# Both heads of a pair at once on TensorE: attention's value products and retention of a two-layer hybrid mixer

## Chip, cores and metric

The kernel runs on one core of one Trainium2 chip. The metric is the device time of one execution in microseconds (us).

## What is computed

A two-layer encoder over 512 tokens of width 1024, in fp32. Each layer is half a SwiGLU feed-forward network (FFN), then a mixer of four parallel groups of 256 channels (short convolution, an RWKV-7 recurrence in both directions, retention, latent attention) whose outputs w_out joins, then half of another FFN. The change touches retention and attention; both have 4 heads of 64 channels:

```python
# retention, per head: chunks qc, kc, vc of q, k (roped) and v
scores = jnp.einsum('bhnid,bhnjd->bhnij', qc, kc) * intra_decay[None, :, None]
o = jnp.einsum('bhnij,bhnjd->bhnid', scores, vc)
...
o = (o + dec_start * jnp.einsum('bhnid,nbhde->bhnie', qc, R_f)
     + dec_end * jnp.einsum('bhnid,nbhde->bhnie', qc, R_b))
...
# attention, per block of queries
sc = jnp.einsum('bqhd,bkhd->bhqk', qn, k_nope) + jnp.einsum('bqhr,bkr->bhqk', qr, k_rope)
p = jax.nn.softmax(sc.astype(jnp.float32) * scale, axis=-1)
return jnp.einsum('bhqk,bkhd->bqhd', p.astype(v.dtype), v)
```

## The kernel before

Activations lie with channels on the 128 partitions and the 512 tokens along the free axis. FFN and projections split each fp32 operand into two parts of a faster type and make three products (lines 338 to 340); the products inside the mixers are plain fp32 and go over the array twice.

`Mixers.run` writes a layer's mixer down as: RWKV's projections, its inverse, its recurrence (`rwkv_chain`, 8 steps of two chunks), attention's latents, the convolution, retention's projections, attention of heads 0 and 1 (`mla(0)`), retention, RWKV's norm, attention of heads 2 and 3 (`mla(1)`), w_out. A scheduler then orders each engine's instructions by priorities and by its own model of time; so the recurrence's short products (lines 1043 to 1107) are spread over the stretch, and PE does the other mixers' products between them. PE and the other engines take their instructions strictly in the order that results. `in_turn` ties a list of calls together so that they are issued in that order; the recurrence uses it to alternate between heads or directions that lie on different halves of the array.

A product of heads in retention or attention fills only a part of the 128x128 array. Retention works on heads 2j and 2j+1 (the pair j) in partitions 0 to 63 and 64 to 127. Its 512 tokens are two halves (c) of 256, each of two tiles (s) of 128. Per pair:

- keys are transposed (line 609) and scaled by decay on DVE (611); `ret_sp`, the states of both halves, is 8 products of 128 rows by 64 columns (619), copied to `st` (623);
- head by head, half by half: scores `ret_ps` (634), 2 products of 64 rows by 128 columns and 256 tokens; DVE multiplies by the decay (636) into `ret_ms`; into `ret_po` go the product of queries with the state (639, 64 rows by 64 columns) and two products of values with `ret_ms` (642, 128 rows by 64 columns, head e on column half e).

`mla` goes head by head too: scores `m_sc` (775), softmax on DVE and ACT (777 to 782), transposes `m_ptp` (787) to four tiles `m_pT` (788), then four products with values (792, 128 rows by 64 columns, 512 tokens) into `m_po`, copied to its half of `y` (793). The accumulators of a head's products (PSUM tiles) come from three tags: "mm" has 3 banks, "a" 2, "b" 3; retention uses "mm" alone, heads 2 and 3 of attention use all three. The tiles `m_pT` and `ret_ms` come from the pool "f" of 23.

Of the kernel before, what the change touches and what calls it, by code (L numbers as in the profile page):

```python
# [9 lines left out]
F32R = mybir.dt.float32r  # L10
# [5 lines left out]
P = 128  # L16
# [3 lines left out]
NT = T // P  # L20
# [7 lines left out]
MLA_TAGS = (("mm", "mm", "mm"), ("mm", "mm", "mm"), ("b", "a", "mm"), ("b", "a", "mm"))  # L28
H = 4
N = 64  # L30
# [382 lines left out]
class Mixers:  # L413
# [179 lines left out]
    def retention(self):  # L593
        k, l, nc, V, A, G = self.k, self.l, self.nc, self.nc.vector, self.nc.scalar, self.nc.gpsimd
        mm = nc.tensor.matmul
        q, kk, vv = self.rq, self.rk, self.rv
        kdt, _ = CON["kd"]
        outs = []
        for j in range(2):
# [8 lines left out]
            for tt in range(NT):  # L608
# [2 lines left out]
            V.tensor_tensor(kn.rearrange("p (t h d) -> p t h d", t=NT, h=2), pt.rearrange("p (t h d) -> p t h d", t=NT, h=2),  # L611
                            tab.unsqueeze(3).to_broadcast([P, NT, 2, N]), ALU.mult)
            sps = k.ps("ret_sp", "mm")
            for e in range(2):
                h = 2 * j + e
                for d in range(2):
                    for s in range(2):
                        tt = 2 * d + s
                        mm(sps[64 * e:64 * e + 64, N * d:N * d + N],
                           kn[:, P * tt + 64 * e:P * tt + 64 * e + 64], vv(tt)[:, N * h:N * h + N],  # L620
                           start=s == 0, stop=s == 1)
            st = big[:, 768:896]
            V.tensor_copy(st, sps[:, 0:2 * N])
            po = k.ps("ret_po", "mm")
            for e in range(2):
                h = 2 * j + e
                r = slice(64 * e, 64 * e + 64)
                for c in range(2):
                    i = slice(256 * c, 256 * c + 256)
                    ms = k.ft("ret_ms")  # L630
                    ps = k.ps("ret_ps", "mm")
                    for s in range(2):
                        jt = 2 * c + s
                        mm(ps[:, 256 * s:256 * s + 256], kk[j][r, P * jt:P * jt + P], q[j][r, i], start=True, stop=True)
                    for s in range(2):
                        V.tensor_tensor(ms[:, 256 * s:256 * s + 256], ps[:, 256 * s:256 * s + 256],
                                        toe[e][:, 128 - 128 * s:384 - 128 * s], ALU.mult)

                    mm(po[r, i], st[r, N * (1 - c):N * (1 - c) + N], qd[r, i], start=True, stop=False)
                    for s in range(2):  # L640
                        jt = 2 * c + s
                        mm(po[r, i], vv(jt)[:, N * h:N * h + N], ms[:, 256 * s:256 * s + 256],
                           start=False, stop=s == 1)
            o, sq = k.ft("ret_o"), k.ft("ret_sq")
            V.tensor_tensor(o, po, self.rg[j], ALU.mult)
            A.activation(sq, po, AF.Square)
# [113 lines left out]
    def mla(self, j):  # L760
        k, l, nc, V, A = self.k, self.l, self.nc, self.nc.vector, self.nc.scalar
        mm = nc.tensor.matmul
        ident = k.con("ident")
        fq, v = self.fq, self.mv
        for h in (2 * j, 2 * j + 1):
            e = h % 2
            if e == 0:
                y = k.ft("m_y")
            qT, kT = self.qT[h], self.kT[j][:, e]
            tag = MLA_TAGS[h]  # L770
            pp = [k.ht("m_p") for _ in range(2)]
# [12 lines left out]
            for kt in range(NT):  # L784
# [1 line left out]
                for qt in range(NT):  # L786
                    nc.tensor.transpose(pt[:, P * qt:P * qt + P], pp[qt // 2][:, qt % 2, P * kt:P * kt + P], ident)
                (A.copy if kt % 2 else V.tensor_copy)(pT[kt], pt)
            po = k.ps("m_po", tag[2])
            r = slice(64 * e, 64 * e + 64)  # L790
            for kt in range(NT):
                mm(po[r], v[:, kt, N * h:N * h + N], pT[kt], start=kt == 0, stop=kt == NT - 1)  # L792
            (A.copy if e else V.tensor_copy)(y[r], po[r])
            if e:
                k.dump(f"ymla{j}_{l}", y)
                self.y_split(6 + j, y, k.vt(f"ys{6 + j}", dt=F32R))


    def rwkv_in(self):
# [460 lines left out]
```

## Time and profile before

| | us |
|---|---|
| median of 3 runs | 2233.18 (2233.13 to 2240.66) |
| the profiled execution | 2230.46 |
| its span, first to last instruction | 2227.9 |
| PE busy | 2171.2 |
| DVE busy | 1142.5 |
| ACT busy | 696.0 |
| POOL busy | 193.5 |
| mean granted clock of TensorE | 0.987 |

PE does the matrix products and transposes, DVE and ACT work through tiles element by element, POOL is a third such engine and SP issues the DMAs. Busy times overlap; the span is the time from the first to the last instruction. The mixer's stretch of the first layer lies at some 370 to 760 us of the span, that of the second at some 1470 to 1860. An fp32 product stands as two rows (passes) in the trace, each with a weight load of its own.

### The profile page before, as it was taken

What the parts mean: (1) busy time and instruction counts of PE and PEld (TensorE: products, weight loads), DVE (VectorE), ACT (ScalarE), POOL (GpSimd) and SP (SyncE); (2) the same over time, 40 slices, a digit from 0 to 9 for tenths busy, and PEclk for the clock granted to TensorE, in tenths of its full rate; (3) what the DMA queues carried; (4) which work ended last, traced back from release to release, by engine and by line L of the source; (5) the groups of instructions that cost most, each with busy time, mean ns of one, the idle gap of its engine ahead of it and who ended that gap; (6) DMA issues with size and microseconds to landing.
All of it is one profiled execution on the core that took longest, in us unless ns stands there. A gap on an engine that the chain in (4) does not pass through costs nothing.

```text
span 2227.9 us, 27585 instructions
## 1 busy us (share of the span) xinstructions
PE 2171.2 (97%) x11332; PEld 1732.9 (78%) x11332; DVE 1142.5 (51%) x1905; ACT 696.0 (31%) x1035; POOL 193.5 (9%) x176
## 2 busy tenths in 40 slices
PE   8999999999999999999999999999999999999997
PEld 7888888777765888888888888887776568888886
DVE  4454345587467643443543344447856765344333
ACT  4322233432233422232322222334223243222232
POOL 1000001132110100000100000003121101000001
PEclk9999999989999999999999999999999999999998
DMA  4223224134002322332322232341340113223222
GB/s 166 95 96 108 95 94 148 59 95 131 15 16 71 128 95 84 105 104 77 103 95 95 94 105 95 110 131 60 95 113 15 63 49 122 94 86 113 95 84 77
DMA packets 65294, 204.68 MB, mean 92 GB/s; under 512 B 26512, under 2 KB 26768, under 8 KB 50960
## 3 DMA queue, kind: packets, MB, share of 16 engines
q1 hardware_dynamic: 65168, 202.93, 27.7%
q8 instruction: 88, 1.44, 0.3%
q14 instruction: 38, 0.31, 0.0%
HBM read 191.37 MB, written 9.44 MB: 90 GB/s over the span
## 4 chain that ended last, share of the span: by engine, by line
PE 84%; DVE 9%; DMA 2%; ACT 2%; SPq 1%; issue 1%; POOL 0%; DVEq 0%; ACTq 0%; POOLq 0%
PE pg L340 7%; PE pg L338 7%; PE pg L339 7%; PE pu L338 7%; PE pu L339 7%; PE pd L339 7%; PE pd L340 7%; PE pu L340 7%; PE pd L338 7%; DVE w_lo L328 2%; PE m_po L792 1%; DVE Rb L958 1%; PE po L338 1%; PE po L340 1%; PE pj L338 1%
## 5 line engine op out<-in xcount | busy, mean ns | idle before, releaser
L327 ACT CAST w_hi<-w_raw 128x1024 fp32r<-128x1024 f32 (+4 forms) x446 | 367.4, 836 | 1133.6 <-PE pg L339 309.2
L328 DVE TENSOR_TENSOR w_lo<-w_raw,w_hi 128x1024 fp32r<-128x1024 f32 (+4 forms) x446 | 434.1, 981 | 215.5 <-ACT w_hi L327 206.9
L338 PE MATMUL pg<-xg,w_hi 128*128 128x512 f32 x704 | 275.4, 391 | 6.0 <-ACT w_hi L327 6.0
L340 PE MATMUL pg<-xg,w_lo 128*128 128x512 f32 x704 | 274.9, 390 | 0.6 <-DVE w_lo L328 0.5
L339 PE MATMUL pg<-xg,w_hi 128*128 128x512 f32 x704 | 275.0, 391 | 0.0
L338 PE MATMUL pu<-xg,w_hi 128*128 128x512 f32 x704 | 274.1, 389 | 0.5 <-ACT w_hi L327 0.5
L339 PE MATMUL pu<-xg,w_hi 128*128 128x512 f32 x704 | 274.2, 389 | 0.0
L340 PE MATMUL pu<-xg,w_lo 128*128 128x512 f32 x704 | 274.1, 389 | 0.0
L340 PE MATMUL pd<-g,w_lo 128*128 128x512 f32 x704 | 273.9, 389 | 0.0
L338 PE MATMUL pd<-g,w_hi 128*128 128x512 f32 x704 | 273.9, 389 | 0.0
L339 PE MATMUL pd<-g,w_hi 128*128 128x512 f32 x704 | 273.9, 389 | 0.0
L372 DVE TENSOR_TENSOR g<-pu,s 128x512 f32<-128x512 f32 x88 | 60.8, 691 | 274.2 <-PE pu L340 271.4
L288 POOL TENSOR_TENSOR acc<-acc,sq 128x512 f32<-128x512 f32 x48 | 65.5, 1364 | 1521.7 <-ACT sq L286 1521.3
L369 DVE TENSOR_TENSOR s<-pg,rb 128x512 f32<-128x512 f32 x88 | 60.8, 691 | 206.4 <-PE pg L340 206.3
L340 PE MATMUL pj<-xg,w_lo 128*128 128x512 f32 x368 | 149.5, 408 | 13.4 <-DVE w_lo L328 13.3
L338 PEld LDWEIGHTS pg<-xg,w_hi 128*128 128x128 f32 x704 | 132.6, 188 | 33.9 <-ACT w_hi L327 6.2
L340 PEld LDWEIGHTS pg<-xg,w_lo 128*128 128x128 f32 x704 | 132.5, 188 | 29.0 <-DVE w_lo L328 1.8
L339 PEld LDWEIGHTS pg<-xg,w_hi 128*128 128x128 f32 x704 | 132.5, 188 | 28.5 <-DVE xg L274 1.0
L338 PEld LDWEIGHTS pu<-xg,w_hi 128*128 128x128 f32 x704 | 132.2, 188 | 28.2 <-ACT w_hi L327 0.9
L340 PEld LDWEIGHTS pu<-xg,w_lo 128*128 128x128 f32 x704 | 132.2, 188 | 27.6 <-DVE w_lo L328 0.3
L338 PEld LDWEIGHTS pd<-g,w_hi 128*128 128x128 f32 x704 | 132.2, 188 | 27.5
L339 PEld LDWEIGHTS pd<-g,w_hi 128*128 128x128 f32 x704 | 132.2, 188 | 27.5
(293 smaller groups left out, 2893.6 us busy)
## 6 DMA issues: line engine op xcount, KB each, us to landing
w_raw<-gu SPq DMA_DIRECT2D x87, 1024.0 KB, 4.9
w_raw<-dn SPq DMA_DIRECT2D x64, 704.0 KB, 4.1
w_raw<-win SPq DMA_DIRECT2D x22, 1024.0 KB, 5.0
w_raw<-wo SPq DMA_DIRECT2D x32, 256.0 KB, 2.8
xs<-x SPq DMA_DIRECT2D x16, 256.0 KB, 4.7
x<-xs SPq DMA_DIRECT2D x16, 256.0 KB, 5.4
w_raw<-wtv SPq DMA_DIRECT2D x4, 576.0 KB, 4.6
x<-xT SPq DMA_DIRECT2D x8, 256.0 KB, 5.7
```

The costliest lines, as they stand in the source:

```text
L288: nc.gpsimd.tensor_tensor(self.acc, self.acc, self.sq, ALU.add)
L327: self.split_hi = self.nc.scalar.copy(hi[:, s], raw[:, s])
L328: self.nc.vector.tensor_tensor(lo[:, s], raw[:, s], hi[:, s].bitcast(F32), ALU.subtract)
L338: T_.matmul(ps, hi, xh, start=start, stop=False)
L339: T_.matmul(ps, hi, xl, start=False, stop=False)
L340: T_.matmul(ps, lo, xh, start=False, stop=stop)
L369: V.tensor_tensor(s, pg, rb, ALU.mult)
L372: V.tensor_tensor(g, pu, s, ALU.mult)
L792: mm(po[r], v[:, kt, N * h:N * h + N], pT[kt], start=kt == 0, stop=kt == NT - 1)
L958: V.tensor_tensor(Rb[:, 0:t, t:], Rb[:, 0:t, t:], tm, ALU.subtract)
```

## The change

In retention the loops over the pair's heads go inside: the states (line 617 of the changed program), the scores (634) and the values (646) of both heads are issued alternately by `in_turn`, head 0 on one half of the array, head 1 on the other. Each head of the pair has its own bank of scores. The product of queries with the state is made for both heads at once (642), with the two states as diagonal blocks of a 128x128 matrix; POOL sets the other two blocks to zero (625), and DVE copies each head's state in an instruction of its own (626). In attention the value products of a pair (801) come after both heads' transposes and alternate between the heads; one copy of 128 partitions takes the place of two of 64.

```diff
-            for e in range(2):
-                h = 2 * j + e
-                for d in range(2):
-                    for s in range(2):
-                        tt = 2 * d + s
-                        mm(sps[64 * e:64 * e + 64, N * d:N * d + N],
-                           kn[:, P * tt + 64 * e:P * tt + 64 * e + 64], vv(tt)[:, N * h:N * h + N],
-                           start=s == 0, stop=s == 1)
-            st = big[:, 768:896]
-            V.tensor_copy(st, sps[:, 0:2 * N])
+            def state(d, s, e):
+                h, tt = 2 * j + e, 2 * d + s
+                return mm(sps[64 * e:64 * e + 64, N * d:N * d + N], kn[:, P * tt + 64 * e:P * tt + 64 * e + 64],
+                          vv(tt)[:, N * h:N * h + N], start=s == 0, stop=s == 1)
+
+            self.in_turn([(state, d, s, e) for d in range(2) for s in range(2) for e in range(2)])
+
+            st = big[:, 768:1024].rearrange("p (d e n) -> p d e n", d=2, e=2)
+            for e in range(2):
+                r = slice(64 * e, 64 * e + 64)
+                G.memset(st[r, :, 1 - e], 0.0)
+                V.tensor_copy(st[r, :, e], sps[r, 0:2 * N].rearrange("p (d n) -> p d n", d=2))
             po = k.ps("ret_po", "mm")
-            for e in range(2):
-                h = 2 * j + e
-                r = slice(64 * e, 64 * e + 64)
-                for c in range(2):
-                    i = slice(256 * c, 256 * c + 256)
-                    ms = k.ft("ret_ms")
-                    ps = k.ps("ret_ps", "mm")
-                    for s in range(2):
-                        jt = 2 * c + s
-                        mm(ps[:, 256 * s:256 * s + 256], kk[j][r, P * jt:P * jt + P], q[j][r, i], start=True, stop=True)
...
-                    mm(po[r, i], st[r, N * (1 - c):N * (1 - c) + N], qd[r, i], start=True, stop=False)
-                    for s in range(2):
-                        jt = 2 * c + s
-                        mm(po[r, i], vv(jt)[:, N * h:N * h + N], ms[:, 256 * s:256 * s + 256],
-                           start=False, stop=s == 1)
+            for c in range(2):
+                i = slice(256 * c, 256 * c + 256)
+                ps, ms = [k.ps("ret_ps", "mm") for _ in range(2)], [k.ft("ret_ms") for _ in range(2)]
+
+                def scores(s, e):
+                    r, jt = slice(64 * e, 64 * e + 64), 2 * c + s
+                    return mm(ps[e][:, 256 * s:256 * s + 256], kk[j][r, P * jt:P * jt + P], q[j][r, i], start=True, stop=True)
+
+                self.in_turn([(scores, s, e) for s in range(2) for e in range(2)])
+                for e in range(2):
...
+                mm(po[:, i], st[:, 1 - c].rearrange("p e n -> p (e n)"), qd[:, i], start=True, stop=False)
+
+                def values(s, e):
+                    h, jt = 2 * j + e, 2 * c + s
+                    return mm(po[64 * e:64 * e + 64, i], vv(jt)[:, N * h:N * h + N], ms[e][:, 256 * s:256 * s + 256],
+                              start=False, stop=s == 1)
+
+                self.in_turn([(values, s, e) for s in range(2) for e in range(2)])
...
-            po = k.ps("m_po", tag[2])
-            r = slice(64 * e, 64 * e + 64)
-            for kt in range(NT):
-                mm(po[r], v[:, kt, N * h:N * h + N], pT[kt], start=kt == 0, stop=kt == NT - 1)
-            (A.copy if e else V.tensor_copy)(y[r], po[r])
-            if e:
-                k.dump(f"ymla{j}_{l}", y)
-                self.y_split(6 + j, y, k.vt(f"ys{6 + j}", dt=F32R))
+            pTs.append(pT)
+
+        po = k.ps("m_po", MLA_TAGS[2 * j + 1][2])
+
+        def values(kt, e):
+            o = N * (2 * j + e)
+            return mm(po[64 * e:64 * e + 64], v[:, kt, o:o + N], pTs[e][kt], start=kt == 0, stop=kt == NT - 1)
+
+        self.in_turn([(values, kt, e) for kt in range(NT) for e in range(2)])
+        (A.copy if j else V.tensor_copy)(y, po)
+        k.dump(f"ymla{j}_{l}", y)
+        self.y_split(6 + j, y, k.vt(f"ys{6 + j}", dt=F32R))
```

The scheduler makes a new order of the whole stretch. Three places on PE's queue, in the first layer (a product is one row here, x3 is three equal ones in a row; lines behind the change are moved by up to ten).

From heads 0 and 1's last transposes to the first pair's first scores, before:

```order
L787 MATMUL m_ptp<-con_t,m_p 128x128 x4
L792 MATMUL m_po<-m_pT,m_v 64x512 x3
L609 MATMUL ret_pt<-con_t,ro_t 128x128 x4
L1089 MATMUL zy_3764<-ch_3762 64x64 x2
L1089 MATMUL zy_3765<-ch_3763 64x64 x2
L1089 MATMUL zy_3764<-ch_3762 64x64 x2
L1089 MATMUL zy_3765<-ch_3763 64x64 x2
L792 MATMUL m_po<-m_pT,m_v 64x512
L619 MATMUL ret_sp<-ret_v,ret_big 64x64 x8
L634 MATMUL ret_ps<-ro_t 128x256 x2
```

and now:

```order
L793 MATMUL m_ptp<-con_t,m_p 128x128 x4
L801 MATMUL m_po<-m_pT,m_v 64x512 x5
L609 MATMUL ret_pt<-con_t,ro_t 128x128 x4
L801 MATMUL m_po<-m_pT,m_v 64x512 x3
L1099 MATMUL zy_3764<-ch_3762 64x64 x2
L1099 MATMUL zy_3765<-ch_3763 64x64 x2
L1099 MATMUL zy_3764<-ch_3762 64x64 x2
L1099 MATMUL zy_3765<-ch_3763 64x64 x2
L617 MATMUL ret_sp<-ret_v,ret_big 64x64 x8
L634 MATMUL ret_ps<-ro_t 128x256 x4
```

Head 1's four value products were the rows of 3 and 1 (head 0's stood some 55 rows earlier); the eight of both heads are the rows of 5 and 3, and the scores are four, of both heads.

The first pair's two halves, from the product with the state to the next piece of the recurrence, before:

```order
L639 MATMUL ret_po<-ret_big 64x256
L634 MATMUL ret_ps<-ro_t 128x256 x2
L642 MATMUL ret_po<-ret_ms,ret_v 64x256 x2
L639 MATMUL ret_po<-ret_big 64x256
L634 MATMUL ret_ps<-ro_t 128x256 x2
L1062 MATMUL zy_3840<-Sd,KQ_2516 128x128
```

and now:

```order
L642 MATMUL ret_po<-ret_big 128x256
L646 MATMUL ret_po<-ret_ms,ret_v 64x256
L634 MATMUL ret_ps<-ro_t 128x256
L646 MATMUL ret_po<-ret_ms,ret_v 64x256 x3
L634 MATMUL ret_ps<-ro_t 128x256 x3
L642 MATMUL ret_po<-ret_big 128x256
L1072 MATMUL zy_3840<-Sd,KQ_2516 128x128
```

Four value products of a half stand as one and three, and so do the next half's scores.

Heads 2 and 3 at the start of w_out (`po`), from transposes of head 2 to the last value products, now:

```order
L793 MATMUL m_ptp<-con_t,m_p 128x128 x6
L256 MATMUL ret_pb<-con_t,ret_sq 128x128 x8
L801 MATMUL m_po<-m_pT,m_v 64x512
L793 MATMUL m_ptp<-con_t,m_p 128x128 x2
L1170 MATMUL py_5329<-con_t,gn_wk 128x128 x2
L338 MATMUL po<-ys_5178,w_hi 128x512 x2
L1170 MATMUL py_5330<-con_t,gn_wk 128x128 x2
L793 MATMUL m_ptp<-con_t,m_p 128x128 x8
L801 MATMUL m_po<-m_pT,m_v 64x512 x4
L339 MATMUL po<-ys_5178,w_hi 128x512
```

Before, their value products stood as four groups of 2, each behind its own transposes; now they are groups of 1, 4 and, ten products of w_out later, 3.

## Rows read from the trace of the kernel before

**Rows 1.** The page: the chain that ended last, by engine.

```profile
PE 84%; DVE 9%; DMA 2%; ACT 2%; SPq 1%; issue 1%; POOL 0%; DVEq 0%; ACTq 0%; POOLq 0%
```

**Rows 2.** Table by stage, first layer: start:end us, length, then as its heading says.

```profile
core 0: us, PE busy (x) PEld busy (x) DVE busy (x) ACT busy (x) POOL busy (x), PEclk, DMA share, GB/s
605.00:645.00 40.00, 39.93 (x345) 23.90 (x340) 26.24 (x65) 16.43 (x37) 5.63 (x12) 1.00 0.00 1
645.00:679.00 34.00, 33.36 (x275) 20.89 (x273) 23.01 (x61) 7.21 (x14) 7.12 (x7) 1.00 0.23 75
679.00:693.00 14.00, 10.38 (x32) 4.48 (x32) 13.62 (x51) 5.79 (x14) 1.32 (x1) 0.88 0.18 66
693.00:760.00 67.00, 66.92 (x296) 50.40 (x295) 42.40 (x72) 28.38 (x47) 9.66 (x7) 1.00 0.28 95
```

**Rows 3.** Waits of PE, 605 to 693 us: total us, times, longest us.

```profile
PE m_sc L775 <- ACT m_p L780: 3.5, 2, 3.2
PE zy L1107 <- DVE ch L1077: 0.6, 1, 0.6
```

**Rows 4.** By tile, both layers: ns of one (min/median/max), first and last start.

```profile
L792 PE MATMUL m_po<-m_pT,m_v x64: 592/592/643, 624.7 to 1813.1; 128*64 128x512 f32 x64
...
L634 PE MATMUL ret_ps<-ro_t x64: 376/376/480, 646.2 to 1770.3; 64*128 64x256 f32 x64
```

**Rows 5.** Timeline of PE: start us, us until its last end, line, shape, count.

```profile
644.80 0.59 PE L792 MATMUL m_po<-m_pT,m_v 128*64 128x512 f32 x1
...
645.23 0.59 PE L792 MATMUL m_po<-m_pT,m_v 128*64 128x512 f32 x1
645.24 1.05 PE L619 MATMUL ret_sp<-ret_v,ret_big 128*64 128x64 f32 x15
646.22 1.13 PE L634 MATMUL ret_ps<-ro_t 64*128 64x256 f32 x4
```

**Rows 6.** Timeline of PE, first pair of heads: one head's groups one after another.

```profile
649.11 1.13 PE L634 MATMUL ret_ps<-ro_t 64*128 64x256 f32 x4
650.17 1.08 PE L642 MATMUL ret_po<-ret_ms,ret_v 128*64 128x256 f32 x4
651.17 0.64 PE L639 MATMUL ret_po<-ret_big 64*64 64x256 f32 x2
651.75 1.13 PE L634 MATMUL ret_ps<-ro_t 64*128 64x256 f32 x4
```

**Rows 7.** Timeline of PE: groups that already alternate between two halves of the array.

```profile
631.55 0.69 PE L1089 MATMUL zy<-ch 128*64 128x64 f32 x16
632.16 1.99 PE L775 MATMUL m_sc<-m_kT,m_qT 128*128 128x512 f32 x4
...
635.85 1.16 PE L1043 MATMUL psG<-KQ,KB 64*128 64x128 f32 x16
636.94 0.71 PE L1062 MATMUL zy<-Sd,KQ 128*128 128x128 f32 x4
```

**Rows 8.** Timeline of PE: line 642 on one half of columns, line 619 on the other.

```profile
659.71 0.27 PE L619 MATMUL ret_sp<-ret_v,ret_big 128*64 128x64 f32 x1
659.74 0.38 PE L642 MATMUL ret_po<-ret_ms,ret_v 128*64 128x256 f32 x1
...
659.95 0.38 PE L642 MATMUL ret_po<-ret_ms,ret_v 128*64 128x256 f32 x1
...
660.17 0.38 PE L642 MATMUL ret_po<-ret_ms,ret_v 128*64 128x256 f32 x1
```

**Rows 9.** DVE and POOL in the first layer, by line and by tile.

```profile
L636 DVE TENSOR_TENSOR ret_ms<-ret_ps,ret_big 128x256 f32<-128x256 f32 x16 | 6.0, 416 | 3.7 <-PE ret_ps L634 3.7
...
L1099 DVE TENSOR_TENSOR Sd<-ch,Pm 128x256 f32<-128x256 f32 x4 | 1.7, 467 | 0.0
...
L623 DVE COPY ret_big<-ret_sp x2: 279/286/292, 646.3 to 661.2; 128x128 f32<-128x128 f32 x2
...
L1102 POOL TENSOR_TENSOR Sc<-ch,Pd 128x128 f32<-128x128 f32 x2 | 1.2, 612 | 7.7 <-DVE ch L1098 7.7
```

More of the change, by code (lines that the diff above doesn't have):

```diff
@@ L624, in retention @@
-            po = k.ps("ret_po", "mm")
-            for e in range(2):
-                h = 2 * j + e
-                r = slice(64 * e, 64 * e + 64)
-                for c in range(2):
-                    i = slice(256 * c, 256 * c + 256)
-                    ms = k.ft("ret_ms")
-                    ps = k.ps("ret_ps", "mm")
-                    for s in range(2):
-                        jt = 2 * c + s
-                        mm(ps[:, 256 * s:256 * s + 256], kk[j][r, P * jt:P * jt + P], q[j][r, i], start=True, stop=True)
-                    for s in range(2):
-                        V.tensor_tensor(ms[:, 256 * s:256 * s + 256], ps[:, 256 * s:256 * s + 256],
-                                        toe[e][:, 128 - 128 * s:384 - 128 * s], ALU.mult)
-                    mm(po[r, i], st[r, N * (1 - c):N * (1 - c) + N], qd[r, i], start=True, stop=False)
-                    for s in range(2):
-                        jt = 2 * c + s
-                        mm(po[r, i], vv(jt)[:, N * h:N * h + N], ms[:, 256 * s:256 * s + 256],
-                           start=False, stop=s == 1)
+            def state(d, s, e):
+                h, tt = 2 * j + e, 2 * d + s
+                return mm(sps[64 * e:64 * e + 64, N * d:N * d + N], kn[:, P * tt + 64 * e:P * tt + 64 * e + 64],
+                          vv(tt)[:, N * h:N * h + N], start=s == 0, stop=s == 1)
@@ new lines, in retention @@
+            self.in_turn([(state, d, s, e) for d in range(2) for s in range(2) for e in range(2)])
+            st = big[:, 768:1024].rearrange("p (d e n) -> p d e n", d=2, e=2)
+            for e in range(2):
+                r = slice(64 * e, 64 * e + 64)
+                G.memset(st[r, :, 1 - e], 0.0)
+                V.tensor_copy(st[r, :, e], sps[r, 0:2 * N].rearrange("p (d n) -> p d n", d=2))
+            po = k.ps("ret_po", "mm")
+            for c in range(2):
[6 more added lines that the diff above has]
+                for e in range(2):
+                    for s in range(2):
+                        V.tensor_tensor(ms[e][:, 256 * s:256 * s + 256], ps[e][:, 256 * s:256 * s + 256],
+                                        toe[e][:, 128 - 128 * s:384 - 128 * s], ALU.mult)
+                mm(po[:, i], st[:, 1 - c].rearrange("p e n -> p (e n)"), qd[:, i], start=True, stop=False)
[4 more added lines that the diff above has]
+                self.in_turn([(values, s, e) for s in range(2) for e in range(2)])
@@ L764, in mla @@
         fq, v = self.fq, self.mv
+        y = k.ft("m_y")
+        pTs = []
         for h in (2 * j, 2 * j + 1):
             e = h % 2
-            if e == 0:
-                y = k.ft("m_y")
             qT, kT = self.qT[h], self.kT[j][:, e]
```

## Prediction

> **What bounds the kernel now.** I read the chain of waits first: TensorE (PE) carries 84% of the chain that ended last [rows 1], so a microsecond of PE work is worth a microsecond wherever PE doesn't wait. Then the table by stage, for the stretch in which the changed products run. From 605 to 679 us PE is busy for 73.3 of 74 us, from 693 to 760 for 66.9 of 67, at a granted clock of 1.00 (2.4 GHz); only from 679 to 693 does it stand still, for 3.6 us, while DVE is busy for 13.6 of 14 us and the granted clock is 0.88 in the mean, so part of it 1.2 GHz after the standstill [rows 2]. PE's waits say the same: 0.6 us on DVE and 3.5 us on ACT's softmax between 605 and 693 us [rows 3]. So the recurrence's steps never wait for their own latency: other PE work, ours among it, fills every gap. The second layer repeats this some 1,100 us later. The reader is to see that this stretch is bound by the PE queue, with a softmax stall at its end that belongs to DVE and ACT.
>
> Next, what a product costs. An fp32 product makes two passes over the array: 16 value products a layer, in two layers, are 64 rows [rows 4]. A pass of 512 columns starts 0.43 us after the one before (644.80, 645.23) [rows 5]; one of 256 columns 0.215 us after (659.74, 659.95, 660.17) [rows 8]. A group of passes of another shape also pays for opening: four passes of line 634 hold PE for 1.06 us, four of 642 for 1.00, two of 639 for 0.58, against 0.86, 0.86 and 0.43 of passes, so 0.20, 0.14 and 0.15 us a group [rows 6].
>
> Last, whether two halves of the array do work at the same time here. Line 1089 alternates column halves: 16 passes of 64 columns take 0.61 us, 0.038 each, where line 619's 15 that don't alternate take 0.98, 0.065 each [rows 7, 5]. Line 1043 alternates row halves: 16 passes of 128 columns in 1.09 us, 0.068 each, where half of a 256-column pass would be 0.107 [rows 7, 8]. And line 642 on one column half keeps its 0.215 us while line 619 runs on the other [rows 8]. So a pair costs one pass. I call that a slot.
>
> **The change, part by part, for one layer.** The order of the changed program decides how many pairs are formed: the scheduler cuts groups of four into one and three. A lone product takes 2 slots, three alternating ones 4 (the half that has two of them decides), four take 4, five take 6.
> - Attention's values: 32 passes become groups of 5 and 3 (first pair of heads), and of 1, 4 and 3 (second), so 6+4+2+4+4 = 20 slots. 12 passes of 0.43 us go: 5.2 us, half of it after 693 us, where PE is just as full [rows 2].
> - Retention's scores: 32 passes become groups of 4, 1, 3, then 1, 3, 1, 3: 22 slots. Ten of 0.215 us: 2.2 us.
> - The product with the state (line 639): 8 products over a quarter of the array become 4 over all of it, 16 passes become 8: 1.7 us.
> - Retention's values: 32 passes become four times 1 and 3: 24 slots: 1.7 us.
> - The state (line 619): 1.0 us becomes line 1089's 0.6 for the first pair [rows 5, 7]; for the second it already ran half beside line 642 [rows 8], so nothing. 0.4 us.
> - Openings: 32 groups of these products become 24. Other groups (transposes, scores of the recurrence) are split in the new order; I count half of the eight, at 0.15 us: 0.6 us.
>
> Sum 11.8 us a layer, **23.6 us** in both.
>
> What it adds: one more DVE copy of 0.29 us for each pair of heads (two of 64 partitions for one of 128) and two memsets of zero blocks on POOL, bounded by nothing and by the nearest POOL row, 0.6 us each [rows 9]. The order puts at least the group of scores and a piece of the recurrence between them and the product that reads them, over 1.5 us of PE work, so I cost both at nothing; without that cover it would be 1.5 us a pair of heads, 6 us in all. Fewer evacuations of attention's output (two of 128 partitions a layer, not four of 64) save DVE and ACT some 0.6 us each, beside the PE work.
>
> What can be late next: the values wait for DVE's multiplies by the decay, 0.416 us each [rows 9], now four for both heads, 1.7 us, and behind them on PE's queue stands the recurrence. The scores of the second half also need the banks that the first two of these free. Before, one head's group ran while DVE worked on the other's. Between scores and values there now stand the product with the state, 0.6 us, and mostly a piece of the recurrence, 0.6 to 1.2 us. Uncovered rest: between nothing and 0.8 us in each of the 8 groups of both layers (two pairs, two halves). I take 0.15 us, nearer to nothing because PE never waited for such a multiply before: 1.2 us in all. Holding the first head's four transposed tiles until the second's are ready costs only space; its products move back behind the second head's transposes.
>
> Net: 22.4 us. The profiled execution took 2230.46 us, 2227.9 of them the span and 2.6 around it, so it would take 2208.1. It stands 2.7 us below the median of the runs shown, 2233.18; from that the forecast is **2211 us**. About 0.5%, 11 us, is what a measurement of this kernel can tell from no change.
>
> **One rule against the trace.** In the rows the weight loads of one column half don't hold up the other: line 642's passes keep their 0.215 us while line 619 starts a pass every 0.06 us beside them, each with a load of its own [rows 8]. The Trainium skill ("TensorE: Matmul & The Clock Gate", Part 3, packing small matmuls) states that a weight load overlaps matmuls in flight only where its row group differs. Both column halves use all rows, so by that rule the value products would gain nothing, and the time would be the second rival's. The trace does not agree with it, at least for short passes beside long ones; two long passes on two column halves stand in no row.
>
> **The rivals.**
> (1) DVE takes over. From 645 to 693 us it is busy for 36.6 of 48 us [rows 2]. If what PE gains there only lengthens the stall for the softmax and the group norm, the retention's gain is lost and only the attention values' 5.2 us a layer stay: 2233.2 - 10.4 = 2223 us. For it: 13.6 of 14 us busy at the end. Against it: 11.4 us of DVE's 48 are free, more than is taken out there (some 6.6), and its work there is fed by the same PE queue, so it moves forward too. Chance 0.12.
> (2) Long passes on two column halves don't run at once; only row halves do, and the short state passes. Then the values gain nothing: 2.2 + 1.7 + 0.4 + 0.6 = 4.9 us a layer, 2233.2 - 9.8 = 2223 us. Against it: [rows 7, 8]. Chance 0.05.
> (3) Slower: PE's queue stands before the values in each of the 8 groups until DVE has done the four multiplies and what is queued before them, say five chain operations of 0.467 us [rows 9]: 1.7 + 2.3 = 4.0 us, 32 in all, less the 22.4 + 1.2 gained: 2233.2 + 8.4 = 2242 us. It decides from 23.6 / 8 = 2.95 us of idle a group on. Against it: 1.2 to 1.8 us of PE work stand between, and DVE has gaps of its own. Chance 0.04.
>
> **How the numbers follow.** My forecast has 0.79. Range: at the lower end every opening counts (1.2 us), nothing is uncovered (1.2 us) and the softmax stall shrinks by half because its scores come earlier (3.6 us in both layers), with the 2.7 us between profile and median: 2202. At the upper end the additions are uncovered (6 us) and the multiplies at 0.8 us (5.2 us more): 2222, which leaves out most of the rivals and little else. Faster by over 0.5% means below 2222: the forecast nearly whole (0.78) and half of (1) and a third of (2), together 0.85. Within 0.5%: the rest of these, 0.11. Slower: 0.04.
>
> **What would show it.** Right: in the values (lines 801 and 646 now) two passes start together and pairs follow 0.43 and 0.215 us apart; the table by stage shows the recurrence's end some 8.6 us earlier in the first layer (2.6 of attention's values, 6.6 of retention, less 0.6 of waits) and the end of w_out some 11.2, with PE's waits as before. Wrong: new waits of PE on the multiplies (line 639 now); a stall after the recurrence that is longer than 3.6 us by what the groups have lost; passes on two column halves at 0.43 us one after another.

## The result, and the profile after

The changed kernel takes **2207.0 us** (2204.9 to 2209.9 in four runs) against 2233.2 (2232.8 to 2240.7): a ratio of 0.9876 with a 95% interval of 0.9852 to 0.9900. The forecast was 2211, with 2202 to 2222. The profiled execution took 2204.9 us, 25.6 less than that of before.

Four marks on PE's timeline divide the stretch in both layers: A, the first scores of attention (line 775 before, 781 after); R, the last pass of the recurrence's last step (1107; 1117); W, the first product of w_out (338, `po`); E, the last one. R to W is the stall.

| | A, us | A to R | R to W | W to E | A to E |
|---|---|---|---|---|---|
| before, layer 1 | 608.9 | 69.7 | 14.0 | 56.1 | 139.7 |
| before, layer 2 | 1708.5 | 69.7 | 15.0 | 55.3 | 140.0 |
| after, layer 1 | 607.6 | 62.7 | 11.7 | 53.2 | 127.6 |
| after, layer 2 | 1696.4 | 62.7 | 11.7 | 53.2 | 127.6 |

So 12.2 and 12.4 us went in the stretch (differences in this document are taken from unrounded times), against 11.2 a layer in the forecast (9.2 - 0.6 up to R, nothing in the stall, 2.6 behind it). The remaining 1.0 of the 25.6 lies outside, where no instruction was changed.

The page of the changed kernel, busy times and chain:

```profile
PE 2148.4 (98%) x11316; PEld 1724.3 (78%) x11316; DVE 1141.4 (52%) x1907; ACT 694.1 (32%) x1033; POOL 197.3 (9%) x184
...
PE 85%; DVE 10%; DMA 1%; SPq 1%; ACT 1%; issue 1%; DVEq 0%; ACTq 0%
```

PE is busy for 22.8 us less than before and still carries 85% of the chain [rows 1]. The table by stage in the first layer, cut at the new R and W:

```profile
core 0: us, PE busy (x) PEld busy (x) DVE busy (x) ACT busy (x) POOL busy (x), PEclk, DMA share, GB/s
605.00:645.00 40.00, 39.67 (x370) 25.00 (x370) 28.25 (x70) 17.21 (x38) 6.43 (x14) 1.00 0.01 2
645.00:671.00 26.00, 24.95 (x225) 15.55 (x224) 22.29 (x59) 5.21 (x11) 5.99 (x5) 1.00 0.29 93
671.00:685.00 14.00, 10.92 (x42) 5.82 (x43) 13.94 (x49) 6.64 (x15) 1.27 (x1) 1.00 0.20 75
685.00:748.00 63.00, 63.00 (x291) 49.07 (x291) 40.78 (x72) 27.99 (x45) 9.64 (x7) 1.00 0.30 101
```

PE is full outside the stall, as it was [rows 2], but for the wait shown next; DVE is full in the stall; the granted clock there is now 1.00 where it was 0.88. PE's waits from 605 to 685 us:

```profile
PE m_sc L781 <- ACT m_p L786: 2.9, 2, 1.7
PE ret_po L646 <- DVE ret_ms L639: 1.0, 1, 1.0
```

Of the 0.6 us that the recurrence waited for DVE [rows 3] nothing is left. A wait of 1.0 us on the multiplies by the decay is new, and there is one of it, not eight. The groups, on PE's timeline (start us, us until the last end, line, shape, count):

```profile
636.45 2.79 PE L801 MATMUL m_po<-m_pT,m_v 128*64 128x512 f32 x10
639.17 0.66 PE L609 MATMUL ret_pt<-con_t,ro_t 128*128 128x128 f32 x4
...
641.87 0.22 PE L617 MATMUL ret_sp<-ret_v,ret_big 128*64 128x64 f32 x1
641.87 0.22 PE L1099 MATMUL zy<-ch 128*64 128x64 f32 x1
...
642.55 1.14 PE L634 MATMUL ret_ps<-ro_t 64*128 64x256 f32 x8
643.61 0.69 PE L1117 MATMUL zy<-ch,Gm 128*64 128x64 f32 x16
...
646.87 0.65 PE L646 MATMUL ret_po<-ret_ms,ret_v 128*64 128x256 f32 x2 [1.05 <-DVE ret_ms L639]
647.45 0.70 PE L634 MATMUL ret_ps<-ro_t 64*128 64x256 f32 x2
648.07 1.08 PE L646 MATMUL ret_po<-ret_ms,ret_v 128*64 128x256 f32 x6
649.08 1.13 PE L634 MATMUL ret_ps<-ro_t 64*128 64x256 f32 x6
650.14 0.70 PE L642 MATMUL ret_po<-ret_big 128*128 128x256 f32 x2
```

Ten value passes of 512 columns (five products) hold PE for 2.72 us, up to the next row: six slots of 0.43 and an opening. Eight score passes take 1.06 (four slots), six value passes of retention 1.01 (four), two alone 0.58 to 0.62 (two). These are the slots of the prediction. In the ten, the two of a pair start 0.01 us apart and pairs follow every 0.43 us. Passes of two lines on the two column halves even stand with one and the same start (641.87).

The stall, before (line numbers of before):

```profile
678.14 0.69 PE L1107 MATMUL zy<-ch,Gm 128*64 128x64 f32 x16 [0.64 <-DVE ch L1077]
...
679.66 2.11 PE L775 MATMUL m_sc<-m_kT,m_qT 128*128 128x512 f32 x4
...
686.05 1.86 PE L775 MATMUL m_sc<-m_kT,m_qT 128*128 128x512 f32 x2 [3.20 <-ACT m_p L780]
688.23 1.85 PE L775 MATMUL m_sc<-m_kT,m_qT 128*128 128x512 f32 x2 [0.32 <-ACT m_p L780]
...
692.56 0.50 PE L338 MATMUL po<-ys,w_hi 128*128 128x512 f32 x1
```

and after:

```profile
668.83 1.12 PE L781 MATMUL m_sc<-m_kT,m_qT 128*128 128x512 f32 x2
669.89 0.69 PE L1117 MATMUL zy<-ch,Gm 128*64 128x64 f32 x16
...
676.61 1.12 PE L781 MATMUL m_sc<-m_kT,m_qT 128*128 128x512 f32 x2 [1.68 <-ACT m_p L786]
...
680.58 1.12 PE L781 MATMUL m_sc<-m_kT,m_qT 128*128 128x512 f32 x2 [1.24 <-ACT m_p L786]
...
682.00 0.50 PE L338 MATMUL po<-ys,w_hi 128*128 128x512 f32 x1
```

Three things differ. A second score product of head 2 (668.83) stands ahead of the recurrence's last step, in the place of the 0.64 us wait; before, 14 of the 16 score passes of heads 2 and 3 stood behind R, now 12. The waits for softmax are 1.68 and 1.24 us, not 3.20 and 0.32. And the product after the wait takes 1.12 us, not 1.86: the mean granted clock from R to W is 1.00 in both layers, where it was 0.88 and 0.89.

### The profile page after: what moved, and what is told of

Read it like the earlier page. It is cut to its first block, busy times and chain, and to the rows that moved or that the text cites. A ratio compares the mean times of both kernels' runs of the same rounds, so it can differ in the third digit from the quotient of the medians.

```text
span 2203.1 us, 27577 instructions
## 1 busy us (share of the span) xinstructions
PE 2148.4 (98%) x11316; PEld 1724.3 (78%) x11316; DVE 1141.4 (52%) x1907; ACT 694.1 (32%) x1033; POOL 197.3 (9%) x184
## 4 chain that ended last, share of the span: by engine, by line
PE 85%; DVE 10%; DMA 1%; SPq 1%; ACT 1%; issue 1%; DVEq 0%; ACTq 0%
PE pg L338 7%; PE pg L340 7%; PE pg L339 7%; PE pu L338 7%; PE pd L339 7%; PE pu L339 7%; PE pd L340 7%; PE pd L338 7%; PE pu L340 7%; DVE w_lo L328 2%; PE po L338 1%; PE po L339 1%; PE po L340 1%; DVE Rb L968 1%; PE pj L338 1%
```

## Experiments

The table has them all; times of two layers stand as first/second. "Left" is how many of the 16 score passes of heads 2 and 3 stand behind R. Each ratio is taken against runs of the kernel before on the same chip, whose medians lay between 2233.2 and 2235.8; so ratios compare better than medians.

| kernel | median us | ratio to before (95%) | A to R | R to W | W to E | left |
|---|---|---|---|---|---|---|
| before | 2233.2 | | 69.7/69.7 | 14.0/15.0 | 56.1/55.3 | 14 |
| after | 2207.0 | 0.9876 (0.9852 to 0.9900) | 62.7/62.7 | 11.7/11.7 | 53.2/53.2 | 12 |
| e1 attention only | 2223.2 | 0.9953 (0.9938 to 0.9968) | 67.4/67.4 | 13.4/14.3 | 53.6/53.3 | 14 |
| e2 retention only | 2213.4 | 0.9911 (0.9897 to 0.9926) | 64.6/64.6 | 10.9/10.5 | 56.4/56.4 | 12 |
| e3 head after head | 2226.8 | 0.9970 (0.9958 to 0.9983) | 66.1/66.1 | 14.1/14.3 | 56.1/55.7 | 14 |
| e5 state by quadrants | 2206.2 | 0.9876 (0.9859 to 0.9892) | 61.9/61.6 | 12.1/12.0 | 53.3/53.3 | 12 |
| e4 whole groups | 2211.6 | 0.9898 (0.9873 to 0.9923) | 61.5/61.5 | 15.2/15.8 | 53.5/52.9 | 14 |
| e6 second pair by head | 2215.1 | 0.9916 (0.9891 to 0.9941) | 62.7/64.4 | 11.6/11.6 | 55.8/55.8 | 12 |
| e9 scaling on ACT | 2207.7 | 0.9879 (0.9857 to 0.9901) | 62.7/62.7 | 10.9/10.9 | 53.6/53.7 | 12 |
| e10 e4 and e9 | 2206.5 | 0.9875 (0.9854 to 0.9896) | 61.5/61.6 | 13.1/13.1 | 52.8/52.8 | 14 |
| e13 roots on POOL | 2210.2 | 0.9885 (0.9870 to 0.9901) | 62.7/62.7 | 13.6/13.6 | 51.8/51.9 | 12 |
| e14 before, roots on POOL | 2232.5 | 0.9988 (0.9977 to 0.9999) | 69.6/69.6 | 13.6/15.7 | 56.8/55.5 | 14 |
| e15 e9 and e13 | 2204.4 | 0.9865 (0.9848 to 0.9883) | 62.7/62.7 | 10.6/10.6 | 53.3/53.3 | 12 |
| e16 second score after R | 2213.8 | 0.9905 (0.9891 to 0.9919) | 62.5/62.5 | 15.2/16.7 | 52.8/52.0 | 14 |

### The two parts alone

The kernel before with attention's edit alone:

```diff
...
-            for kt in range(NT):
-                mm(po[r], v[:, kt, N * h:N * h + N], pT[kt], start=kt == 0, stop=kt == NT - 1)
...
+        self.in_turn([(values, kt, e) for kt in range(NT) for e in range(2)])
...
```

> Only attention's value products are issued for both heads in turn; retention stays as before. PE-bound theory (a pair costs one pass, and what leaves PE's queue leaves the time): groups of 5 and 3 for the first pair of heads, so 10 passes' time for 16 there, and much the same for the second pair: some 11 passes of 0.43 us a layer, 4.7 us, so about 2233 - 9.5 = 2223 us. If long passes on two column halves don't run at once: 2233 us, and ten passes of line 801's first group take 4.4 us in place of 2.7. If DVE and the softmax end the stage: only the second pair's half shows, about 2228 us.

2223.2 us, as slots say: 2.2 us less up to R and 2.0 to 2.5 behind W in each layer. Its two stalls were granted different clocks. Table by stage, R to W of the first and the second layer:

```profile
674.70:688.10 13.40, 9.10 (x41) 4.23 (x35) 13.30 (x47) 5.57 (x14) 1.79 (x1) 1.00 0.23 81
1773.80:1788.10 14.30, 10.22 (x41) 5.05 (x35) 13.83 (x51) 5.73 (x13) 1.60 (x1) 0.88 0.20 75
```

The same products of PE at full clock and at 0.88 in the mean: 13.4 and 14.3 us. DVE is the full engine in both, but starts four instructions more in the second (46 and 50 from R to W). The difference is not shown to be the clock's: the two stalls of the kernel before differ by 1.0 us as well, at 0.88 and 0.89. From R to E this kernel takes 3.1 us less than the kernel before in the layer where the clock is back at 1.00, and 2.8 in the other. So in a stall that DVE fills the lower clock is seen to cost some 0.4 us at E, by this one pair of stretches.

Retention's edit alone (the same for states and values, and line 642 for both heads):

```diff
...
-                    for s in range(2):
-                        jt = 2 * c + s
-                        mm(ps[:, 256 * s:256 * s + 256], kk[j][r, P * jt:P * jt + P], q[j][r, i], start=True, stop=True)
...
+                self.in_turn([(scores, s, e) for s in range(2) for e in range(2)])
...
```

> Only retention works on both heads in turn; attention's value products stay head by head. PE-bound theory: 56 slots of 0.215 us a layer where there were 80, and 1 us for the state and openings, less 0.6 us of waits on the multiplies: 5.6 us a layer, about 2222 us; the recurrence ends some 5.6 us earlier in each layer. If DVE ends the stage, the recurrence ends earlier as well, but the start of w_out does not: 2231 to 2233 us. Also read here: whether the granted clock in the stall after the recurrence falls as before (0.88 in the mean) or stays at 1.00 as with the whole change.

2213.4 us, 8.6 below the expectation. Up to R it saves 5.1 us a layer. The surplus is the stall: 10.9 and 10.5 us, with 12 score passes left as in the changed kernel, and with waits that are short (PE's waits, first layer):

```profile
PE po L338 <- ACT m_p L786: 1.4, 1, 1.4
PE m_sc L781 <- ACT m_p L786: 1.0, 2, 0.6
PE m_ptp L793 <- DVE m_p L788: 0.5, 2, 0.3
```

A to E the parts save 5.4/5.0 and 7.9/8.5 us, 13.2/13.5 together, and the whole 12.2/12.4: they add up but for 1 us a layer. So most of what the forecast had missed comes with retention (attention alone shortens the stall by 0.6 and 0.7 us), and lies behind R.

### Do the halves work by themselves?

All of head 0's products of a group ahead of head 1's, the rest as changed:

```diff
...
-                self.in_turn([(scores, s, e) for s in range(2) for e in range(2)])
+                self.in_turn([(scores, s, e) for e in range(2) for s in range(2)])
...
-        self.in_turn([(values, kt, e) for kt in range(NT) for e in range(2)])
+        self.in_turn([(values, kt, e) for e in range(2) for kt in range(NT)])
```

> The whole change, but all of head 0's products of a group are issued before head 1's. It tells how far the two halves are independent. If each half takes its own passes in order and only looks past the other's, four scores in a row (two of each head) still take 4 passes' time, 1.06 us, and six value products (four and two) 8 passes of 0.43 us, 3.6 us: about 2218 us in all, since the scheduler cuts the other groups between the heads. If passes start strictly in the order of the queue, four scores take 7 passes' time, 1.7 us, six value products 11, 4.9 us: about 2225 us.

```profile
637.22 3.70 PE L801 MATMUL m_po<-m_pT,m_v 128*64 128x512 f32 x12
640.86 0.66 PE L609 MATMUL ret_pt<-con_t,ro_t 128*128 128x128 f32 x4
...
644.35 1.14 PE L634 MATMUL ret_ps<-ro_t 64*128 64x256 f32 x8
645.42 0.69 PE L1117 MATMUL zy<-ch,Gm 128*64 128x64 f32 x16
```

Four passes of head 0's scores and then four of head 1's take 1.07 us, as in turn. Twelve value passes, eight of head 0 ahead of four of head 1, take 3.64 us, what head 0's eight need alone; head 1's first starts at 639.00, 0.01 us behind the fifth of head 0 and ahead of its last three, which stand before it in the queue. So a half that is free does start a pass past others, here past three, and a strict order of starts is refuted: that PE takes its instructions strictly in the order of its queue, as said above, is true of starts here only within a half. Yet the time is 2226.8, worse than either theory said: the scheduler cuts a group after one to three products, which here are of one head, and a group with one head in it has no partner (641.44 to 643.21 us: four value passes in three pieces). Issuing in turn is what makes every piece a pair.

### What the additions cost

The product with the state as two of 64x64 in turn, one copy, no memsets:

```diff
...
-                mm(po[:, i], st[:, 1 - c].rearrange("p e n -> p (e n)"), qd[:, i], start=True, stop=False)
+                def cross(e):
+                    r = slice(64 * e, 64 * e + 64)
+                    return mm(po[r, i], st[r, N * (1 - c):N * (1 - c) + N], qd[r, i], start=True, stop=False)
+
+                self.in_turn([(cross, e) for e in range(2)])
```

> The whole change, but the product of queries with the state is two products on two quarters of the array, issued in turn, in place of one over the whole with zero blocks; so the second copy on DVE and the memsets on POOL go. If a pair on two quarters costs one pass as well and the additions were hidden: the same time, 2207 us within 2, and 0.53 to 0.63 us for each such group. If the additions held PE up: up to 6 us faster. If quarters don't run at once: 8 passes of 0.215 us a layer more, 2210.5 us.

```profile
649.14 0.65 PE L641 MATMUL ret_po<-ret_big 64*64 64x256 f32 x4
649.72 0.71 PE L1073 MATMUL zy<-Sd,KQ 128*128 128x128 f32 x4
```

2206.2 us, and 0.58 for two products on two quadrants, what one had taken alone [rows 6]. The time is the same, but not because nothing changes: the wait of 1.0 us on the multiplies is gone in both layers, A to R is 0.8 and 1.2 us shorter, and the stall 0.4 longer. DVE's queue shows why, with the second copy and the memsets:

```profile
643.61 0.58 DVE L626 COPY ret_big<-ret_sp 64x128 f32<-64x128 f32 x2
644.22 0.69 DVE L513 TENSOR_TENSOR ys<-m_y,ys 128x512 fp32r<-128x512 f32 x1
644.83 1.53 DVE L513 TENSOR_TENSOR ys<-c_y,ys 128x512 fp32r<-128x512 f32 x1
646.39 1.42 DVE L639 TENSOR_TENSOR ret_ms<-ret_ps,ret_big 128x256 f32<-128x256 f32 x4
```

and without (e5):

```profile
644.00 0.28 DVE L623 COPY ret_big<-ret_sp 128x128 f32<-128x128 f32 x1
644.20 0.69 DVE L513 TENSOR_TENSOR ys<-m_y,ys 128x512 fp32r<-128x512 f32 x1
644.81 0.68 DVE L513 TENSOR_TENSOR ys<-c_y,ys 128x512 fp32r<-128x512 f32 x1
645.41 1.40 DVE L636 TENSOR_TENSOR ret_ms<-ret_ps,ret_big 128x256 f32<-128x256 f32 x4
```

The copies take 0.3 us more on DVE ahead of the multiplies. So the subtraction of line 513 for the convolution's output starts later against POOL, which makes a product of RWKV's norm at the time. POOL's row in the changed kernel, and in e5:

```profile
644.57 1.25 POOL L1146 TENSOR_TENSOR gn_wk<-vn,bon 128x512 f32<-128x512 f32 x1 [0.62 <-PE zy L1117]
...
644.96 1.43 POOL L1147 TENSOR_TENSOR gn_wk<-vn,bon 128x512 f32<-128x512 f32 x1 [0.62 <-DVE ys L513]
```

In the changed kernel the subtraction starts 0.26 us behind POOL's product, ends 0.55 behind its end, and takes 1.53 us; in e5 it starts 0.15 us ahead of it and takes 0.68. In every run with the wait of 1.0 us this subtraction takes 1.53 us, in both layers; in those without the wait it takes 0.68, in e3 1.20 (e2 has the second copy as well; its subtraction starts 0.07 us ahead of POOL's product, and nothing waits). So the copy and the memsets hold up nothing that reads them, as costed, but the copy has a part in the new wait. That POOL is what holds DVE there is read from these times; no run moves POOL's product alone.

### What shortened the stall

Attention's second pair head by head, all else as changed:

```diff
-        self.mla(1)
+        self.mla_by_head(1)
```

(`mla_by_head` is `mla` of the kernel before.)

> The changed kernel with attention of heads 2 and 3 head after head as before; retention and heads 0 and 1 stay in pairs. 16 passes take the place of 10 slots: 2.6 us a layer behind the stall. If the parts only add up, 2207 + 5.2 = 2212 us, with the stall after the recurrence as in the changed kernel. The two parts run alone gave 4.6 us more than the whole together. If the second pair's pairing is what spoils the stall (head 2's value products no longer stand there as filler), the stall is 0.7 to 1.2 us a layer shorter here, as in the run of retention alone: about 2210. If the overlap is the first pair's (PE earlier, DVE not), the stall stays and the time is 2212.

2215.1 us, where 2212 was expected if the stall stayed. W to E grows by the 2.6 us of its slots, the stall stays at 11.6: its pairing has no part in it. (A to R takes 1.6 us more in the second layer than in the first, with a spell at 1.2 GHz in it: the mean granted clock from 1700 to 1764 us was 0.97, in the first layer 1.00, and the waits are the same. There PE is full.)

Retention's groups chained, so that fewer are cut:

```diff
...
-                self.in_turn([(scores, s, e) for s in range(2) for e in range(2)])
+                self.in_turn([(scores, s, e) for s in range(2) for e in range(2)], end if c else None)
...
-                self.in_turn([(values, s, e) for s in range(2) for e in range(2)])
+                end = self.in_turn([(values, s, e) for s in range(2) for e in range(2)])
```

> The changed kernel with retention's groups chained to one another (the second half's scores and the next pair's transposes are issued only after the last values), so that the scheduler cuts fewer of them into one and three: scores go from 22 to 18 slots a layer, values from 24 to 18, that is ten slots of 0.215 us or 2.15 us a layer, and five openings of about 0.15 us fewer. If PE's queue alone sets the time, 2.9 us a layer go: about 2201 us, with the recurrence's end 2.9 us earlier. If the stall after the recurrence is set by DVE, which is busy there without a break, it ends with DVE's remaining work and not with PE's: the recurrence ends earlier but the stall grows by part of what was gained, and the time lies between 2203 and 2207. If the chaining exposes the state's and the multiplies' latency (transposes, DVE scaling, state, copy in one line), new waits show on them: 2207 to 2210.

```profile
648.62 1.74 PE L647 MATMUL ret_po<-ret_ms,ret_v 128*64 128x256 f32 x8 [1.05 <-DVE ret_ms L640]
650.29 1.13 PE L635 MATMUL ret_ps<-ro_t 64*128 64x256 f32 x8
...
667.67 1.12 PE L782 MATMUL m_sc<-m_kT,m_qT 128*128 128x512 f32 x2
...
676.62 1.12 PE L782 MATMUL m_sc<-m_kT,m_qT 128*128 128x512 f32 x2 [2.27 <-ACT m_p L787]
```

2211.6 us, above all that was expected. Up to R 1.3 us went, not 2.9. The first whole group of values holds PE for 1.67 us instead of 1.0: DVE does its four multiplies from 648.14 to 649.56, so they aren't done when the group starts. The cut into one and three had hidden that. And the stall is 15.2/15.8 us, with 14 score passes left: one score product has moved behind R again.

Is it the amount of DVE's work that stands in the stall? From R to W DVE starts 51 and 55 instructions before, 37 after. Five kernels take work from DVE: softmax's last scaling of heads 2 and 3 to ACT (e9), the same with whole groups (e10), the iterations of the reciprocal roots to POOL (e13, and e14 on the kernel before), both (e15).

```diff
-                V.tensor_scalar(p, p, sm[:, 3:4], None, ALU.mult)
+                if j:
+                    A.activation(p, p, AF.Copy, scale=sm[:, 3:4])
+                else:
+                    V.tensor_scalar(p, p, sm[:, 3:4], None, ALU.mult)
```

> The changed kernel with the softmax's last scaling of heads 2 and 3 (0.47 us each on DVE, eight a layer) on ACT, which is busy for 6.6 of the 14 us around the stall. Four of them stand on DVE between the recurrence's end and the first product of w_out, 1.9 us. If DVE's work sets the length of the stall, it shrinks by up to 1.9 us a layer: 2203 us, at the same granted clock. If the stall is the latency of one softmax after the other (scores, maximum, exponential, scaling, transposes) or PE's own restart after standing still, an ACT instruction of about 0.6 us in place of DVE's 0.47 changes nothing or costs up to 1 us a layer: 2207 to 2209.

> Whole groups in retention and the scaling on ACT at once. If DVE's work sets the end of the stall, the relief of DVE lets the whole groups' gain through: 2207 - 5.7 - 3.8 = about 2198 us. If the two are independent and only add up as measured alone, the sum of the two runs' differences.

```diff
-            V.tensor_tensor(t, r, r, ALU.mult)
-            V.scalar_tensor_tensor(t, t, -0.5, v, ALU.mult, ALU.mult)
-            V.scalar_tensor_tensor(out if i == 2 else r, t, 1.5, r, ALU.add, ALU.mult)
+            G.tensor_tensor(t, r, r, ALU.mult)
+            G.tensor_tensor(t, t, v, ALU.mult)
+            G.tensor_scalar(t, t, -0.5, 1.5, ALU.mult, ALU.add)
+            G.tensor_tensor(out if i == 2 else r, t, r, ALU.mult)
```

> The changed kernel with the iterations of the reciprocal roots in retention's and RWKV's norms on POOL (12 instructions in place of 9 on DVE for each root). In the changed kernel 10 such small instructions stand on DVE between the recurrence's end and w_out's first product and take 1.6 of its 11.65 us there; some 7 of them move. If DVE's remaining work sets the stall's length, the stall falls to about 10.6 us and the time to 2205 us. If the stall is a chain of softmax latencies, whatever else DVE does, it stays at 11.6 us: 2207 us. If POOL's longer chain now comes last (RWKV's norm before w_out's last products), there is a wait on POOL's results after the stall: 2208 to 2212.

> The kernel before with the same iterations on POOL. Here 21 such instructions stand on DVE between the recurrence's end and w_out's first product, 2.7 of 14.0 us in the first layer and 3.1 of 15.0 in the second; about 16 of them move. If DVE's remaining work sets the stall's length, it falls to about 12 and 13 us, near that of the changed kernel (11.65), and the time by 4 to 5 us: about 2229 against 2233 to 2235. That would show that the stall of the kernel before was longer by DVE's small instructions and not by the lower granted clock. If it was the clock or the softmax's latency, the stall stays at 14 to 15 us, and the time within 1 us.

> The changed kernel with both reliefs of DVE: softmax's last scaling of heads 2 and 3 on ACT, the roots' iterations on POOL. With the scaling alone the stall was 10.9 us, and 19 small instructions of the roots (2.0 us) stood in it; about 15 of these move. If DVE's work sets the length, the stall falls to about 9.3 us and the time to about 2204 us; if what is left there is the softmax's own latency, it stays near 10.9 us and the time at 2207.

The amount alone doesn't decide. None of the times that followed from DVE's amount came (2203, 2198, 2205, 2229), but for e15's 2204, and its stall was 10.6 us, not 9.3. On the kernel before, 37 and 43 instructions of DVE in place of 51 and 55 leave the stall at 13.6 and 15.7 us (e14, ratio 0.9988); in the first layer DVE is idle for 1.3 us of it. In e13 the stall is longer than in the changed kernel, partly because the new order puts transposes, line 256's products and a value product ahead of W: R to E is 65.5 us against 64.8. The scaling gives 0.7 us of the stall (e9) where 1.9 was expected, and 0.5 of it is lost again behind W; together with the roots it gives 1.0 (e15). With whole groups it gives 2.1 and 2.7 (e10 against e4). There DVE's work does count, or the clock: the mean granted clock from R to W is 1.00 in e10, 0.90 and 0.89 in e4.

The last column sorts the kernels. From R to E, with 2.6 us added where the second pair is in turn, those with 12 passes left take 66.5 to 68.1 us, those with 14 take 68.5 to 71.4. But 1.0 us of that is the score product itself, and the clock goes the same way: from R to W it is 1.00 wherever 12 are left. Without the 1.0 us, stretches with 14 left take 67.5 to 69.2 us where the clock is 1.00 (e1's first layer, e3, e10) and 69.1 to 70.4 where it is lower, so e10's lies among those with 12. The last run ties this one product:

```diff
...
-                mm(sc, qT[:, sl], kT, start=True, stop=True)
+                with self.tc.issue_after(self.sums.ins) if (h, qt) == (2, 1) else nullcontext():
+                    mm(sc, qT[:, sl], kT, start=True, stop=True)
```

(`self.sums` is the last product of line 665, which stands behind R.)

> The changed kernel, with the second score product of head 2 tied behind retention's sums of squares, so that it comes after the recurrence's last step, as it stood in the kernel before. All else on PE's queue up to there keeps its order. From the recurrence's end to the end of w_out the changed kernel takes 64.8 us, the kernel before 70.1 and 70.3; 2.6 of the difference are the second pair's value products and 1.0 is the score product itself, which leaves 1.7 to 1.9 us a layer. If these come from that product's place (its softmax starts earlier on DVE and ACT, so that the next scores find their bank sooner), this kernel's recurrence ends 1.0 us earlier and the stretch behind takes about 67.6 us: 2207 + 3.5 = about 2210.5, with waits of 4 us or more in the stall in place of 3.1, and a granted clock of 1.2 GHz in it may come back. If the place of the product is no cause, the stretch takes 65.8 us and the time stays 2207.

```profile
670.58 0.69 PE L1118 MATMUL zy<-ch,Gm 128*64 128x64 f32 x16 [0.70 <-DVE ch L1088]
...
677.06 1.12 PE L782 MATMUL m_sc<-m_kT,m_qT 128*128 128x512 f32 x2 [1.92 <-ACT m_p L787]
...
679.87 3.50 PE L782 MATMUL m_sc<-m_kT,m_qT 128*128 128x512 f32 x4 [0.74 <-ACT m_p L787]
```

2213.8 us, ratio 0.9905. Three things of the kernel before are back: the recurrence's last step waits 0.70 us for DVE, so that R comes only 0.3 us earlier for a product of 1.0; R to E takes 68.0/68.8 us (67.6 expected); and four passes of scores take 3.50 us, at the lower clock. A to E is 2.9 and 3.7 us longer than in the changed kernel. So much is shown for tying this product behind R together with what follows from it. The place alone is not shown to be worth that: the scheduler makes a new order of PE and DVE behind R (line 256 comes ahead of W), and the mean granted clock from R to W is 0.89 and 0.80 instead of 1.00. The runs don't keep the three apart, nor do they show why the scheduler puts the product ahead of R once retention is short.

## Why the prediction was right, step by step

- **Slots: right.** From each pass's start to the next one's on PE's queue, A to R, first layer, by tile (us; the second layer agrees to 0.02):

| | before | after | change | forecast |
|---|---|---|---|---|
| attention's values, first pair | 6.78 | 4.07 | -2.7 | -2.6 |
| retention's scores | 8.46 | 6.11 | -2.4 | -2.2 |
| product with the state, without its wait | 4.41 | 2.40 | -2.0 | -1.7 |
| retention's values | 7.42 | 6.33 | -1.1 | -1.7 |
| states | 2.18 | 1.18 | -1.0 | -0.4 |
| their openings | in the rows above | | | -1.2 |
| waits: multiplies | 0 | 1.05 | +1.05 | +0.6 |
| waits: recurrence's last step | 0.64 | 0 | -0.6 | 0 |
| a second score product ahead of R | | | +0.75 | 0 |
| transposes, line 1053, line 1099, others | | | +1.1 | +0.6 |

  The changed products lose 9.2 us with their openings, where the forecast had 8.6 and 1.2 of openings. (Where passes of two lines alternate, the time from one start to the next goes to the first of the two. Before, this shifts time between values and states; the two together lose 2.1 us, as forecast.)
- **Openings: the step that failed, with the wrong sign.** Of "other groups" the forecast said that they "are split in the new order; I count half of the eight", that is 0.6 us of loss against 1.2 of gain. By the table the gain is 0.6 (9.2 less the 8.6 of slots), and the other groups cost 1.1, 0.4 of it on line 1099, whose passes alternate with the states. So openings cost 0.5 us a layer net instead of giving 0.6. That is 1.1 of the 1.7 us by which R came less early than forecast (6.9, not 8.6); the longer wait on the multiplies is 0.4, and the score product ahead of R 0.75, less the 0.6 of the recurrence's wait.
- **Waits on the multiplies: too much by number, too little by size.** One wait of 1.0 us a layer, at the first group of the first pair; the other three groups don't wait, and in e2 and e5 none does. 2.1 us in both layers, where 1.2 were taken. The forecast set the multiplies' own 1.7 us against PE's work; what made them late was other work ahead of them on DVE's queue, 0.3 us of a second copy and 0.85 by which a subtraction took longer (e5).
- **The stall: mis-sized at zero.** It lost 2.3 and 3.3 us: 1.0 because a score product went ahead of R, the rest, 3.6 us for both layers, with what hangs on that product's place (e16), which isn't resolved further. The lower end of the range had just half of PE's standstill in it (3.6 us for both), as a bound. With the product tied behind R the gain is 9.3 and 8.7 us a layer (e16 against before), below the 11.2 of the forecast. So that the median came within 4 us of the forecast is in part luck: two errors of opposite sign met.
- **w_out: right.** 2.6 us of values (e6 against the changed kernel; from before to after W to E lost 2.9 and 2.1 us).
- **The additions: right for what reads them, not for the queue.** The product with the state never waits for the copy or the memsets. But with the copy comes the wait of 1.0 us on the multiplies, which e5 doesn't have. e5's time is the same within its interval, since the stall takes 0.4 us of the gain back.
- **Rival 1 (DVE takes over): no**, though DVE is busy for 13.94 of the 14 us from 671 to 685; the stall got shorter.
- **Rival 2 (long passes on column halves don't run at once): no.** Ten passes in 2.72 us, where one after another they would take 4.3. The rule of the Trainium skill weighed in the forecast ("TensorE: Matmul & The Clock Gate", Part 3, packing small matmuls), by which loads overlap only with another row group, doesn't hold for these rows either.
- **Rival 3 (a long wait in all eight groups): no.** One group a layer waits, for a third of the idle time at which it would decide.

A version that beats both clearly wasn't found: e15 has the best ratio, 0.9865, within the interval of the changed kernel's, and 126.6 us from A to E against 127.6.

## What to carry to other kernels

Where PE's queue is full, count the passes of a half-array product in slots, per group as the scheduler really cuts it: issued in turn, even a cut group keeps its pairs, and a cut may hide a wait that the whole group would show. Then look at the first place where PE stands still behind the work that was shortened: tying one product of the next stage behind the last dependent step, with the order and the clock that came with it, took back a quarter of the gain here. And look at the whole queue of the engine that a product waits for: a copy of 0.3 us that nothing waits for came with a wait of 1.0 us here. A part's gain measured alone can exceed its share in the whole, so compare stretches between marks in the trace rather than medians.

## What was not expected of the hardware

- A free half of the array starts passes past others that stand ahead in the queue (e3: past three; 12 passes of two heads in the 3.64 us of eight).
- An instruction of DVE that starts while one of POOL runs can take over twice its time: 1.53 us in place of 0.68, ending 0.55 us behind POOL's (line 513 beside line 1146). Where DVE's starts first it is POOL's that takes longer, 1.43 us in place of 1.25 (e5).
- The longest single wait doesn't tell whether the stall sees 1.2 GHz: it did before (3.20 us) and in e4 (2.27 us, 0.90 in the mean from 671 to 686), and did not in e1's first layer (2.91 us). A spell costs 1.6 us where PE is full (e6's second layer), and some 0.4 at E where DVE is (e1 against before, one pair of stretches).
